# A two-layer diffusion trunk on one core: projections of linear attention placed beside its cores, and modulation steps placed later

## The chip, the cores and the metric

The kernel runs on one core of a Trainium2 chip. Its time is the device time of one execution in microseconds (us); the number compared is the median of several runs. A profile, taken by the hardware on one such execution, goes with it. The engines are TensorE (PE, with its weight loads as PEld), VectorE (DVE), ScalarE (ACT), GpSimd (POOL) and SyncE (SP), which issues every DMA of this kernel.

## The reference

Two transformer layers run over 128 context tokens and 1024 latent tokens of width 1024, all in float32. Each token group has its own conditioning vector, and each layer takes six modulation vectors from it, a shift, a scale and a gate for each of two sub-layers:

```
mod = (jax.nn.silu(cond) @ P['w_mod'][li] + P['b_mod'][li])[:, None, :]
shift1, scale1, gate1, shift2, scale2, gate2 = jnp.split(mod, 6, axis=-1)
h = rms_norm(x, g[0]) * (1.0 + scale1) + shift1
out, new = ab_mix(h, ...) if li % 2 == 0 else diff_mix(h, ...)
x = x + gate1 * rms_norm(out, g[1])
h = rms_norm(x, g[2]) * (1.0 + scale2) + shift2
gate, up = jnp.split(h @ P['w_ffn_in'][li], 2, axis=-1)
f = (jax.nn.silu(gate) * up) @ P['w_ffn_out'][li]
x = x + gate2 * rms_norm(f, g[3])
```

In layer 0, `ab_mix` projects h by one matrix `ab_w_in` into the inputs of two attentions, whose outputs are put side by side and projected by `ab_w_out`. One is a latent attention (MLA) with 8 heads: queries and keys/values come out of low-rank vectors of 384 and 256 by "up-projections" (`mla_w_uq`, `mla_w_ukv`), and each query head has a rotated part of 32 and an unrotated part of 64. The other is a gated linear attention (GLA) with 4 heads of 128, run forwards and backwards over chunks of 64 tokens:

```
cum = jnp.cumsum(g, axis=3)
q_in = q * jnp.exp(cum)
k_in = k * jnp.exp(-cum)
a = jnp.where(mask, jnp.einsum('bhncd,bhnsd->bhncs', q_in, k_in), 0.0)
o_intra = jnp.einsum('bhncs,bhnsv->bhncv', a, v)
u = jnp.einsum('bhncd,bhncv->bhndv', k * jnp.exp(cum_last - cum), v)
# S <- decay * S + u from chunk to chunk; o = o_intra + q_in S
```

Layer 1 uses a differential attention on `c_w_qkv`. A feed-forward of width 2816 follows each attention.

## The kernel before

The kernel is written as a list of operations in program order. Every operation is only recorded (`R.tile`, `act`, `dve`, `pe`, `sp`; `Recorder`, from line 171). A planner then sorts the list (`schedule`, line 334): going forward in its own estimate of time, it takes from all operations that are ready, on every engine, the one that can start first, and among equals the one recorded first. The sorted list is issued in `issue` (line 515), whose line 550 is the one line that the profile shows. So each engine executes its instructions in the planner's order. Where a change moves a recorded step, it moves that step's rank, and the planner does the rest.

Memory is handed out by the planner too. A tile belongs to a class ("W", "E", "C", "U", "S", "M", ...), and a class has a fixed list of places in SBUF or banks in PSUM (lines 600 to 635). In most classes tiles get their places strictly in the order in which they are first used in the recorded program. Classes "C" (8 places) and "ps" (8 banks of PSUM) let a later tile go ahead while more than 3, or more than 1, are free. Classes may lie on the same memory, and a place of one is then held back until the other's earlier tiles have been placed (`try_place`, line 377). Four cases matter here:

- "S", 4 places for the states of the linear attention, and "M", 2 places for rows of modulation weights, are the same 2 KB.
- "Uh" (the normalised activations h, six tiles in blocks 0 to 5), "Uq" (MLA inputs, blocks 0 to 4), "Qm" (the attention's queries and keys, blocks 0 to 3) and "U" (the working tiles of the linear attention, blocks 5 to 8) share the nine blocks "U".
- "W" has 4 places for split weights; while the linear attention runs, constants (`gc`, line 1079) and rotation tables (`rq`, line 1090) hold two of them.
- "E" has 6 places; the linear attention's values and output of a head, and the MLA values' output tiles, take them in recorded order.

Float32 products are done in three passes of a faster format: each operand is split into a high and a low part (`load_w`, line 800, does it for weights: DMA into "st", ScalarE copies the high part, VectorE subtracts), and `mm3` multiplies high by high, high by low and low by high. `dense_m` (line 901) makes one 128 x 384 output from 8 blocks of 128 inputs: 24 matmuls. Three such products (3 groups of 384 tokens) go with each weight load.

Layer 0 runs through these stages:

1. Normalised activations h, with two modulation vectors on TensorE (`mod_on_pe`).
2. Projections of h: the output gates of four GLA heads (line 972), the shared rotated key and the GLA gate inputs, the MLA latents (`latent`, line 1011), queries and keys of the four GLA heads (line 1044, stored to DRAM as `qk_d`), and the GLA values for all heads (line 1057).
3. The GLA cores: for each of 4 heads two directions, `gla_core` (line 1153), each over 3 groups of 384 tokens. A group takes a tile of class "U" for its element work on VectorE and ScalarE, then transposes, small matmuls and a chain over the states in class "S". A head's queries and keys take one more "U" tile (`gla_load`, line 1146). After the two directions, `gla_out` (line 1248) normalises, multiplies by the gate and stores.
4. The MLA up-projections are recorded beside the cores: a list `parts` (line 1259) of seven functions (values, rotated queries in two halves, then four times unrotated queries and keys), of which one is recorded after each of the first seven cores. Their inputs are loaded at lines 1092 to 1101.
5. MLA attention, output projection, feed-forward; then layer 1.

The other modulation vectors are computed on VectorE beside all this. `mod_vectors` (line 768) is a generator: for a vector it makes four quarters, each of 8 loads of weight rows (128 x 256) that are multiplied by the conditioning and summed for both token groups, two at a step, followed by a step that transposes and reduces, with a small product on TensorE (tiles `ma`, `mt`). Ten vectors are chained in `later`, in the order (layer, vector) (0,2), (0,4), (0,3), (0,5), (1,1), (1,0), (1,2), (1,4), (1,3), (1,5). `beside(n)` (line 962) records the next n steps at the place in the program where it is called: before each weight load in stage 2, in the products of the feed-forward (line 1614), in two products of its output projection, and before each weight load of layer 1's queries and keys (`diff_qk`, line 1749).

Of the kernel before, what the change touches and what calls it, by code (L numbers as in the profile page):

```python
# [9 lines left out]
F32 = mybir.dt.float32  # L10
F32R = mybir.dt.float32r
AF = mybir.ActivationFunctionType
# [11 lines left out]
GW = 384  # L24
NG = T // GW
# [5 lines left out]
KEYS = NCTX + 128 + NLAT  # L31
# [549 lines left out]
def kernel(ctx: ExitStack, tc: tile.TileContext, I: dict, O: dict):  # L581
    nc = tc.nc
    pool_ = lambda name, bufs, **kw: ctx.enter_context(tc.tile_pool(name=name, bufs=bufs, **kw))
    R = Recorder(nc, tc)
    act, dve, pool, pe, sp = R.act, R.dve, R.pool, R.pe, R.sp
# [62 lines left out]
    def C(dt=F32):  # L648
        return R.tile(now["C"], [128, now["w"]], dt)


    def copy(out, in_):
        R.record([("act", "activation", (), dict(out=out, in_=in_, func=AF.Copy)),
                  ("dve", "tensor_copy", (), dict(out=out, in_=in_))])
# [65 lines left out]
    t = C()[0:64, 0:128]  # L720
# [79 lines left out]
    def load_w(srcs, nk=KD):  # L800

        st = R.tile("st", [128, KD, 128])
        wid = 0
        for off, s in srcs:
            sp.dma_start(out=st[:, 0:nk, off:off + s.shape[1]], in_=s.rearrange("(k p) c -> p k c", p=128))
            wid = max(wid, off + s.shape[1])
        w = R.tile(now["W"], [128, 2, KD, 128], F32R)
        act.activation(out=w[:, 0, 0:nk, 0:wid], in_=st[:, 0:nk, 0:wid], func=AF.Copy)
        tt(w[:, 1, 0:nk, 0:wid], st[:, 0:nk, 0:wid], w[:, 0, 0:nk, 0:wid], ALU.subtract)
        return w  # L810
# [90 lines left out]
    def dense_m(w, h, g, nk=KD, m=128, n=GW):  # L901
        ps = ps_tile()[:m, :n]
        mm3(ps, [((w[:, 0, k, :m], w[:, 1, k, :m]), (h[g][0][:, k, :], h[g][1][:, k, :])) for k in range(nk)])
        return ps
# [57 lines left out]
    def beside(n=1, after=None):  # L962
        R.after = after
        for _ in range(n):
            next(later, None)
        R.after = None
# [3 lines left out]
    start = len(R.ops) - 1  # L970

    for hd in range(4):
        beside(4, start)
        w = first[hd] if hd < FIRST else load_w([(0, W[:, 2240 + hd * 128:2368 + hd * 128])])
        for g in range(NG):
            t = C()
            act.activation(out=t, in_=dense_m(w, h, g), func=AF.Silu)
            sp.dma_start(out=sg_d[hd][:, g * GW:(g + 1) * GW], in_=t)
# [32 lines left out]
    def latent(m0, nk, n, gname, store):  # L1011
        f = [R.tile("E", [128, T]) for _ in range(nk)]
        for m in range(nk):
            beside(5)
            w = load_w([(0, W[:, (m0 + m) * 128:(m0 + m + 1) * 128])])
            for g in range(NG):
                copy(f[m][:, g * GW:(g + 1) * GW], dense_m(w, h, g))
        for g in range(NG):
            s = slice(g * GW, (g + 1) * GW)
            r = norm_r([f[k][:, s] for k in range(nk)], n)  # L1020
            for k in range(nk):
                t = C()
                dve.scalar_tensor_tensor(out=t, in0=f[k][:, s], scalar=vec(gname, k), in1=r,
                                         op0=ALU.mult, op1=ALU.mult)
                store(g, k, t)
# [15 lines left out]
    latent(3, 2, 256, "mla_g_kv", store_kv)  # L1041


    for hd in range(4):
        for i, col in enumerate((672, 1184)):
            beside(5)
            w = load_w([(0, W[:, col + hd * 128:col + (hd + 1) * 128])])
            for g in range(NG):
                t = C()
                if i == 0:  # L1050
                    act.activation(out=t, in_=dense_m(w, h, g), func=AF.Copy, scale=128 ** -0.5)
                else:
                    copy(t, dense_m(w, h, g))
                sp.dma_start(out=qk_d[hd][:, i, g * GW:(g + 1) * GW], in_=t)


    wv = [load_rows([(lambda st: st, W[kk * 256:(kk + 1) * 256, 1696:2208].rearrange("(k p) c -> p k c", p=128))],
# [31 lines left out]

    rq = R.tile("W", [128, 2, NLAT])  # L1090
    sp.dma_start(out=rq, in_=I["k_rope_mla"])
    qn = []
    for g in range(NG):
        q = R.tile("Uq", [128, 2, 3, GW], F32R)
        for j in range(2):
            sp.dma_start(out=q[:, j].bitcast(F32), in_=qn_d[g][j].rearrange("(k p) t -> p k t", p=128))
        qn.append([q[:, j] for j in range(2)])
    ck = [R.tile("Uq", [128, 2, KEYS], F32R) for k in range(2)]
    for k in range(2):
        for j in range(2):  # L1100
            sp.dma_start(out=ck[k][:, j, :].bitcast(F32), in_=ckv_d[j, k * 128:(k + 1) * 128, :])
    Wq = I["mla_w_uq"].rearrange("a (h c) -> a h c", c=96)
    Wk = I["mla_w_ukv"].rearrange("a (h c) -> a h c", c=128)
    qscale = 96 ** -0.5
# [1 line left out]
    def mla_v():  # L1106
        w = load_rows([(lambda st, k=k: st[:, k].rearrange("p (h c) -> p h c", c=64),
                        Wk[k * 128:(k + 1) * 128, :, 64:128]) for k in range(2)], [2, 512])
        for t in range(KEYS // 128):
            s = slice(t * 128, (t + 1) * 128)  # L1110
            ps = ps_tile()
            mm3(ps, [((ck[k][:, 0, s], ck[k][:, 1, s]), (w[:, 0, k, :], w[:, 1, k, :])) for k in range(2)])
            vt = R.tile("E", [128, 8, 2, 64], F32R)
            p3 = ps.rearrange("p (h c) -> p h c", c=64)
            copy(vt[:, :, 0, :], p3)
            dve.tensor_tensor(out=vt[:, :, 1, :], in0=p3, in1=vt[:, :, 0, :], op=ALU.subtract)
            sp.dma_start(out=vm_d[t], in_=vt.rearrange("p a b c -> p (a b c)").bitcast(F32))

    def mla_q_rope(m):
        w = load_w([(32 * i, Wq[:, 4 * m + i, 64:96]) for i in range(4)], nk=3)  # L1120
        for g in range(NG):
            ps = dense_m(w, qn, g, nk=3)
            t = C()
            for c0, n, j in segs(g):
                if j:
                    act.activation(out=t[:, c0:c0 + n], in_=ps[:, c0:c0 + n], func=AF.Copy, scale=qscale)
                else:
                    b = g * GW + c0 - NCTX
                    rope(ps[:, c0:c0 + n], rq[:, 0, b:b + n], rq[:, 1, b:b + n], t[:, c0:c0 + n], qscale)
            hl_to_dram(t, qro_d[m][:, :, g * GW:(g + 1) * GW])  # L1130
# [125 lines left out]
            tt(t, t, sg, ALU.mult)  # L1256
            sp.dma_start(out=mix_d[4 + hd][:, s], in_=t)

    parts = [lambda: mla_v(), lambda: mla_q_rope(0), lambda: mla_q_rope(1)] + [lambda m=m: mla_nope(m) for m in range(4)]
    for hd in range(4):  # L1260
        ld = gla_load(hd)
        for d in range(2):
            gla_core(hd, d, *ld)
            if parts:
                parts.pop(0)()
        gla_out(hd, ld[2])

    HT = NLAT // 2
# [327 lines left out]
    def ffn_in(h, l):  # L1596
# [15 lines left out]
            return out  # L1612

        def product(w, i, acc, first, last=False):
            if l == 0 and i not in ("21", "T3"):
                beside(1, start)
            on = {} if first else {"skip_group_check": True}
            hi, lo = Th[i]
            for u in range(2):
                c = slice(u * 128, (u + 1) * 128)  # L1620
                for k in range(4):
                    wk, a, b = w[k // 2], hi[k // 2][:, k % 2], lo[k // 2][:, k % 2]
                    with R.group():
                        pe.matmul(acc[u], lhsT=wk[:, 0, k % 2, c], rhs=a, start=first and k == 0, stop=False, **on)
                        pe.matmul(acc[u], lhsT=wk[:, 0, k % 2, c], rhs=b, start=False, stop=False, **on)
                        pe.matmul(acc[u], lhsT=wk[:, 1, k % 2, c], rhs=a, start=False, stop=k == 3, **on)
# [120 lines left out]
        sp.dma_start(out=rd[j], in_=I["k_rope_diff"][:, j, :])  # L1747

    def diff_qk(m):
        beside(3)  # L1750
        w = load_w([(0, W[:, m * 128:(m + 1) * 128])])
        scale = 0.125 if m < 8 else 1.0
        for g in range(NG):
            ps = dense_m(w, h, g)
            t = C()
            for c0, n, j in segs(g):
                if j:
                    act.activation(out=t[:, c0:c0 + n], in_=ps[:, c0:c0 + n], func=AF.Copy, scale=scale)
                    if m >= 8:
                        p2 = ps_tile()  # L1760
                        pe.transpose(p2[:, :128], t[:, c0:c0 + n], ident)
                        o = C()
                        copy(o[:, :128], p2[:, :128])
                        sp.dma_start(out=O["new_diff_k"][:, (m - 8) * 128:(m - 7) * 128], in_=o[:, :128])
                else:
                    b = g * GW + c0 - NCTX
                    rope(ps[:, c0:c0 + n], rd[0][:, b:b + n], rd[1][:, b:b + n], t[:, c0:c0 + n], scale)
            if m < 8:
                hl_to_dram(t, q1_d[m][:, :, g * GW:(g + 1) * GW])
            else:  # L1770
                for c0, n, kc in key_cols(g):
                    hl_to_dram(t[:, c0:c0 + n], k1_d[m - 8][:, :, kc:kc + n])
# [195 lines left out]
```

## Time and profile before

| | us |
|---|---|
| median of 3 runs | 3580.55 |
| lowest and highest | 3577.53, 3583.96 |
| the profiled execution's own time | 3575.52 |
| its span in the profile | 3573.7 |
| PE busy in it | 3255.1 (91%) |
| DVE busy | 2506.9 (70%) |
| ACT busy | 1667.5 (47%) |
| mean granted clock of TensorE | 0.944 |

A profile names operations by their tiles: `psum<-U,W` is a matmul whose operands lie in blocks of classes "U" and "W". Names are those of the blocks, so modulation rows show as `S<-in_w_mod` and their sums as `M<-S,sc,M`. "SPq" is a DMA issue on SyncE. In a timeline, the columns are the start, the time that the line covers, the engine, the operation, and behind "x" how many instructions were merged; in square brackets stands how long the engine was idle before, and for whom it waited.

### The profile page before, as it was taken

The numbers are of one execution on the slowest core, as the hardware profiler recorded it, in microseconds if no ns is written. First come the engines' busy times: TensorE is split into PE (matmuls) and PEld (weight loads), VectorE is DVE, ScalarE is ACT, GpSimd is POOL, SyncE is SP. The second block draws the span as 40 slices with busy tenths as digits, with TensorE's granted clock in tenths as the row PEclk, the third lists the DMA queues.
The fourth block names the chain that finished last, engine by engine and source line by source line (L and its number), as shares of the span: only waits on it lengthen the run. The fifth ranks groups of instructions, "written<-read, shape, count | busy, mean of one in ns | idle before, by whom it ended". The sixth has DMA issues, their size and how long they took to land.

```text
span 3573.7 us, 50213 instructions
## 1 busy us (share of the span) xinstructions
PE 3255.1 (91%) x17145; PEld 2773.8 (78%) x17145; DVE 2506.9 (70%) x5941; ACT 1667.5 (47%) x3244; POOL 407.2 (11%) x443
## 2 busy tenths in 40 slices
PE   7999479999876999999998998899997799998997
PEld 5998358889765888877776997788875588887676
DVE  6764577788788877766787587788868755554477
ACT  6422134466565333333455232788856533333344
POOL 0000000133100000000001000566630000000000
PEclk9999678999987999999998999999998799999999
DMA  5455334743343333355345645456333422225224
GB/s 196 134 181 190 121 104 137 200 103 101 114 144 132 124 116 116 117 204 157 106 134 191 188 148 163 102 147 152 111 108 133 128 95 95 92 92 203 84 89 159
DMA packets 359134, 483.49 MB, mean 135 GB/s; under 512 B 39775, under 2 KB 264094, under 8 KB 358206
## 3 DMA queue, kind: packets, MB, share of 16 engines
q1 hardware_dynamic: 358878, 480.29, 43.4%
q8 instruction: 135, 2.21, 0.3%
q14 instruction: 121, 0.99, 0.1%
HBM read 330.42 MB, written 149.77 MB: 134 GB/s over the span
## 4 chain that ended last, share of the span: by engine, by line
PE 80%; DVE 8%; DMA 4%; ACT 4%; issue 2%; POOL 1%; SPq 0%; DVEq 0%; ACTq 0%; POOLq 0%
PE psum L550 80%; DVE U L550 2%; DVE E L550 1%; DVE W L550 1%; ACT E L550 1%; ACT U L550 1%; DMA S<-in_w_mod 1%; DVE C L550 1%; POOL sm L550 1%; POOL E L550 1%; ACT W L550 1%; DVE M L550 1%; DMA C<-hid_d 0%; DVE st L550 0%; DVE H L550 0%
## 5 line engine op out<-in xcount | busy, mean ns | idle before, releaser
L550 PE MATMUL psum<-U,W 128*128 128x512 f32 (+1 forms) x6010 | 1293.7, 370 | 17.2 <-DVE W L550 9.3
L550 PEld LDWEIGHTS psum<-U,W 128*128 128x128 f32 x6010 | 1086.2, 188 | 158.8 <-DVE W L550 11.1
L550 PE MATMUL psum<-E,E 128*128 128x512 f32 x2520 | 588.2, 394 | 28.1 <-ACT E L550 20.2
L550 PEld LDWEIGHTS psum<-E,E 128*128 128x128 f32 x2520 | 475.2, 190 | 133.3 <-ACT E L550 22.0
L550 DVE TENSOR_TENSOR W<-E,W 128x512 fp32r<-128x512 f32 x352 | 240.4, 690 | 185.3 <-ACT W L550 183.2
L550 ACT ACTIVATE E<-E,sm 128x1152 f32<-128x1152 f32 (+1 forms) x280 | 326.8, 1180 | 55.4 <-DVE sm L550 44.6
L550 PE MATMUL psum<-U,U 128*128 128x384 f32 (+4 forms) x1626 | 336.5, 342 | 11.3 <-DVE E L550 3.4
L550 ACT ACTIVATE E<-C 128x512 fp32r<-128x512 f32 (+3 forms) x337 | 197.2, 611 | 318.6 <-PE psum L550 249.2
L550 POOL TENSOR_TENSOR sm<-sm,mhalf 128x1 f32<-128x1 f32 (+2 forms) x124 | 94.4, 766 | 2163.1 <-DVE sm L550 1984.1
L550 ACT ACTIVATE W<-E 128x512 fp32r<-128x512 f32 x352 | 219.3, 628 | 258.2 <-PE psum L550 197.3
L550 DVE TENSOR_TENSOR E<-C,E 128x512 fp32r<-128x512 f32 (+3 forms) x359 | 228.5, 658 | 149.2 <-ACT E L550 147.5
L550 PE MATMUL psum<-W,U 128*128 128x256 f32 (+1 forms) x1620 | 311.7, 339 | 10.2 <-ACT U L550 3.4
L550 DVE TENSOR_SCALAR_CACHE_REDUCE E<-psum 128x384 f32<-128x384 f32 (+1 forms) x600 | 305.7, 538 | 19.2 <-PE psum L550 13.2
L550 PEld LDWEIGHTS psum<-W,U 128*128 128x128 f32 x1620 | 260.0, 195 | 46.4 <-DVE W L550 6.8
L550 DVE SCALAR_TENSOR_TENSOR M<-S,sc,M 128x256 f32<-128x256 f32 x560 | 245.1, 479 | 68.9 <-DMA S<-in_w_mod 51.2
L550 PEld LDWEIGHTS psum<-U,U 128*128 128x128 f32 (+1 forms) x1626 | 265.0, 191 | 32.4 <-DVE E L550 9.6
L550 ACT ACTIVATE C<-psum 128x512 f32<-128x512 f32 (+5 forms) x311 | 128.3, 434 | 342.5 <-PE psum L550 336.2
L550 ACT ACTIVATE W<-psum 128x384 fp32r<-128x384 f32 (+3 forms) x401 | 195.9, 507 | 181.7 <-PE psum L550 175.5
L550 PE MATMUL psum<-ident,E 128*128 128x128 f32 x1273 | 188.7, 286 | 50.0 <-POOL E L550 18.2
L550 PEld LDWEIGHTS psum<-ident,E 128*128 128x128 f32 x1273 | 150.0, 146 | 76.5 <-POOL E L550 29.8
L550 ACT ACTIVATE U<-psum 128x384 f32<-128x384 f32 (+4 forms) x200 | 94.5, 483 | 198.6 <-PE psum L550 192.0
L550 POOL TENSOR_TENSOR E<-E,E 128x1152 f32<-128x1152 f32 (+1 forms) x72 | 174.6, 2426 | 62.8 <-ACT E L550 57.5
(245 smaller groups left out, 3906.7 us busy)
## 6 DMA issues: line engine op xcount, KB each, us to landing
E<-in_w_ffn_in SPq DMA_DIRECT2D x88, 512.0 KB, 3.8
S<-in_w_mod SPq DMA_DIRECT2D x320, 128.0 KB, 2.3
U<-in_w_ffn_out SPq DMA_DIRECT2D x44, 512.0 KB, 6.6
C<-hs_d SPq DMA_DIRECT2D x88, 256.0 KB, 2.6
U<-k_d SPq DMA_DIRECT2D x64, 320.0 KB, 8.5
C<-hid_d SPq DMA_DIRECT2D x66, 256.0 KB, 2.7
st<-in_c_w_qkv SPq DMA_DIRECT2D x24, 512.0 KB, 4.1
st<-in_ab_w_in SPq DMA_DIRECT2D x21, 512.0 KB, 4.0
```

Source lines behind the costliest of these rows:

```text
L550: getattr(self.real[e], m)(*[res(a) for a in args], **{n: res(a) for n, a in kw.items()})
```

## The change

Steps of modulation vectors are recorded at other places (`beside`): 3 instead of 4 before each of the four gate projections, 6 instead of 5 before each of five latent projections, 10 before each of two query and key projections instead of 5 before each of eight, one in six products of a column block of the feed-forward instead of five, and 4 instead of 3 before four of the sixteen weight loads of layer 1.

Of the queries and keys of the linear attention, only head 0's are projected in stage 2. Those of heads 1, 2 and 3 become the first three entries of `parts`, beside the first three cores. The MLA parts follow beside the five later cores, some two at a time, and the loads of their inputs (`mla_in`) move with them.

```
     for hd in range(4):
-        beside(4, start)
+        beside(3, start)
...
         for m in range(nk):
-            beside(5)
+            beside(6)
...
-    for hd in range(4):
-        for i, col in enumerate((672, 1184)):
-            beside(5)
-            w = load_w([(0, W[:, col + hd * 128:col + (hd + 1) * 128])])
-            for g in range(NG):
...
+    def gla_in(hd, i):
+        w = load_w([(0, W[:, (672, 1184)[i] + hd * 128:(672, 1184)[i] + (hd + 1) * 128])])
+        for g in range(NG):
+            t = C()
+            if i == 0:
+                act.activation(out=t, in_=dense_m(w, h, g), func=AF.Copy, scale=128 ** -0.5)
+            else:
+                copy(t, dense_m(w, h, g))
+            sp.dma_start(out=qk_d[hd][:, i, g * GW:(g + 1) * GW], in_=t)
+
+    for i in range(2):
+        beside(10)
+        gla_in(0, i)
...
-    qn = []
-    for g in range(NG):
-        q = R.tile("Uq", [128, 2, 3, GW], F32R)
...
+    qn, ck = [], []
+
+    def mla_in():
+        for g in range(NG):
+            q = R.tile("Uq", [128, 2, 3, GW], F32R)
+            for j in range(2):
+                sp.dma_start(out=q[:, j].bitcast(F32), in_=qn_d[g][j].rearrange("(k p) t -> p k t", p=128))
+            qn.append([q[:, j] for j in range(2)])
+        for k in range(2):
+            t = R.tile("Uq", [128, 2, KEYS], F32R)
+            for j in range(2):
+                sp.dma_start(out=t[:, j, :].bitcast(F32), in_=ckv_d[j, k * 128:(k + 1) * 128, :])
+            ck.append(t)
...
-    parts = [lambda: mla_v(), lambda: mla_q_rope(0), lambda: mla_q_rope(1)] + [lambda m=m: mla_nope(m) for m in range(4)]
+    parts = [[lambda hd=hd, i=i: gla_in(hd, i) for i in range(2)] for hd in range(1, 4)]
+    parts += [[mla_in, mla_v], [lambda: mla_q_rope(0), lambda: mla_q_rope(1)], [lambda: mla_nope(0)],
+              [lambda: mla_nope(1), lambda: mla_nope(2)], [lambda: mla_nope(3)]]
     for hd in range(4):
         ld = gla_load(hd)
         for d in range(2):
             gla_core(hd, d, *ld)
-            if parts:
-                parts.pop(0)()
+            for p in parts.pop(0):
+                p()
         gla_out(hd, ld[2])
...
         def product(w, i, acc, first, last=False):
-            if l == 0 and i not in ("21", "T3"):
+            if l == 0 and i != "21":
                 beside(1, start)
...
     def diff_qk(m):
-        beside(3)
+        beside(4 if m in (0, 1, 8, 9) else 3)
```

More of the change, by code (lines that the diff above doesn't have):

```diff
@@ L1041 @@
     latent(3, 2, 256, "mla_g_kv", store_kv)
-    for hd in range(4):
-        for i, col in enumerate((672, 1184)):
-            beside(5)
-            w = load_w([(0, W[:, col + hd * 128:col + (hd + 1) * 128])])
-            for g in range(NG):
[L1049 to L1054, printed above, removed]
+    def gla_in(hd, i):
[10 more added lines that the diff above has]
+        gla_in(0, i)
     wv = [load_rows([(lambda st: st, W[kk * 256:(kk + 1) * 256, 1696:2208].rearrange("(k p) c -> p k c", p=128))],
@@ L1091 @@
     sp.dma_start(out=rq, in_=I["k_rope_mla"])
-    qn = []
-    for g in range(NG):
-        q = R.tile("Uq", [128, 2, 3, GW], F32R)
[L1095 to L1101, printed above, removed]
+    qn, ck = [], []
[10 more added lines that the diff above has]
+            ck.append(t)
     Wq = I["mla_w_uq"].rearrange("a (h c) -> a h c", c=96)
```

## The prediction, made before the changed kernel was run

> **What bounds the kernel now.** I read the busy slices of the page first, then the busy time in stretches, then TensorE's waits, then the order of time of SyncE and VectorE in the place that these pointed to. In the slices, TensorE is at 7 to 9 tenths nearly everywhere. A slice is 89.3 us (3573.7 / 40); the deepest hole is the fifth, a 4 from 357 to 447, with a 7 behind it. (The other dip, the 6 from 1072 on, is the start of the feed-forward.)
>
> ```profile
> PE   7999479999876999999998998899997799998997
> ```
>
> Cut at the borders of the program's stages, the hole is this (the columns: stretch, length, busy time and instructions of PE, PEld, DVE, ACT, POOL, granted clock, DMA share, GB/s):
>
> ```profile
> 100.00:300.00 200.00, 200.00 (x1238) 194.31 (x1238) 128.41 (x324) 60.44 (x118) 5.97 (x6) 1.00 0.54 161
> 300.00:352.00 52.00, 52.00 (x241) 41.82 (x239) 22.20 (x56) 9.45 (x22) 1.42 (x3) 1.00 0.61 205
> 352.00:365.00 13.00, 10.46 (x44) 7.73 (x42) 9.68 (x23) 7.73 (x15) 0.76 (x3) 1.00 1.02 325
> 365.00:412.00 47.00, 1.38 (x33) 1.03 (x34) 32.61 (x93) 2.72 (x6) 0.00 (x0) 0.50 0.30 92
> 412.00:472.00 60.00, 52.45 (x266) 42.67 (x265) 34.29 (x87) 20.29 (x45) 0.75 (x3) 0.79 0.35 128
> 472.00:545.00 73.00, 57.33 (x255) 43.33 (x255) 51.32 (x141) 25.11 (x56) 4.38 (x10) 0.67 0.24 76
> 545.00:606.00 61.00, 59.65 (x381) 53.18 (x381) 45.73 (x120) 31.90 (x74) 4.10 (x8) 0.94 0.52 165
> 606.00:672.00 66.00, 59.04 (x342) 52.71 (x342) 44.16 (x129) 25.02 (x57) 6.34 (x12) 0.79 0.70 195
> ```
>
> The projections (to 352) fill TensorE wholly at full clock. Then come 47 us with 1.38 us of matmuls. Then the four heads of the linear attention's cores, where TensorE is granted 0.67 to 0.94 of its clock. What ends the 47 us is the group that finishes a quarter of a modulation vector, and behind it stands SyncE's queue:
>
> ```profile
> PE psum L550 <- DVE mt L550: 47.4, 4, 12.3
> ```
>
> ```profile
> 364.97 41.57 SPq L550 DMA_DIRECT2D S<-in_w_mod  x26
> 409.31 0.33 SPq L550 DMA_DIRECT2D S<-in_state_gla_fwd  x1
> 419.17 0.34 SPq L550 DMA_DIRECT2D out_new_gla_fwd<-S  x1
> ```
>
> The initial state of the first core lands in a place that it shares with the weight rows of the modulation steps, and places are handed out in recorded order. All 16 quarters that were recorded ahead of the cores must be through before the first state may be loaded at 409.31. The work recorded behind the first core, the MLA values, can't fill the hole either: their output tiles come after the core's output tile in the order of the E places, so their sums only fill PSUM.
>
> **The steps that move.** A call of `beside` gives one step, five steps finish a quarter, and the first call only starts the chain. Before: 4x4 + 5x5 + 8x5 = 81 calls, which is 16 quarters. After: 4x3 + 5x6 + 2x10 = 62, which is 12 quarters and the first pair of row loads of the thirteenth. The first layer's second gate thus goes behind the cores (it is needed only after the feed-forward), the three vectors that are due earlier stay ahead. The quarters' ends:
>
> ```profile
> 121.30 0.39 DVE L550 TENSOR_REDUCE mt<-ma 128x8 f32<-128x256 f32 x1
> ...
> 331.96 0.42 DVE L550 TENSOR_REDUCE mt<-ma 128x8 f32<-128x256 f32 x1
> ...
> 410.73 0.42 DVE L550 TENSOR_REDUCE mt<-ma 128x8 f32<-128x256 f32 x1
> ```
>
> First, twelfth and sixteenth: (331.96 - 121.30) / 11 = 19.15 us a quarter while TensorE is full. The pace is not set by the number recorded (five calls stand beside a load of some 12.5 us) but by the two places for rows, so fewer projections don't slow it. Quarter 12 still ends at 332; two more row loads, at 41.57 / 26 = 1.6 us each, and their sums make the first state loadable near 337 instead of 409. Bounds: at the stall's pace (12.3 us a quarter, the longest wait above) from the new end of the projections on, 318; a fifth slower, because the first core's element work then shares VectorE, 349.
>
> **The projections that move.** Six pairs of one weight load and three dense products leave the stretch before 352:
>
> ```profile
> L550 SPq DMA_DIRECT2D qk_d<-U x16: 326/327/602, 204.6 to 301.0; - x16
> L550 SPq DMA_DIRECT2D qk_d<-C x8: 320/327/332, 206.7 to 283.9; - x8
> ```
>
> 24 products are stored between 204.6 and 301.0, 96.4 / 23 = 4.2 us each, so 18 products are 75 us. The value projection then ends at 352 - 75 = 277, and from 277 to 337 the first core waits for its state as now. But now there is cover: the queries and keys of heads 1 and 2 (12 products, 50 us) write C places that are next in order, need no E place, and find two of the W places free, as the MLA weights do now. Head 3's (25 us) come behind the output step of head 0 in the order of the C places, so only what PSUM can hold of them is done early. I count the 60 us as full.
>
> What remains from 337 on, in TensorE time at full clock: the cold matmuls cost more, by these rows of the same 12 small products:
>
> ```profile
> 413.26 3.15 PE L550 MATMUL psum<-U 128*64 128x64 f32 x12 [0.58 <-ACT U L550]
> ...
> 453.76 1.94 PE L550 MATMUL psum<-U 128*64 128x64 f32 x12 [0.58 <-ACT U L550]
> ```
>
> 3.15 / 1.94 = 1.62. With a share 2(1 - clock) of each head cold, the heads' busy 52.45, 57.33, 59.65 and 59.04 become 44, 43, 57 and 49.5: 193 us of work in 260, or 0.74. After: 193, plus 10 that the MLA values did at 352 to 365, plus 75 - 60 of the moved projections: 218. At 0.74 that is 293 us, at the best head's 57 / 61 = 0.93 it is 234. I take 0.78, so 279 us: heads 1 to 3 now have more work beside them, but head 0 loses its MLA values and most of its cover, and lies near the worst head (43 / 73 = 0.59). The cores end at 337 + 279 = 616 instead of 672: 56 us less. With 318 or 349 for the state, the same sum gives 622 and 613: when the state comes matters little, since the waiting time is work.
>
> A rule of the Trainium skill speaks against taking cover from a core: "TensorE: Matmul & The Clock Gate", section "What's actually happening", has the array at half rate after a window of some 3.4 us without work. The granted 0.50 in the empty 47 us agrees; the 1.62 above is less than its 2. By 2 instead of 1.62 a wholly cold head 0, with head 1's 43 us of work, would be estimated at 86 us rather than 70, and the gain would be some 16 us less.
>
> **What else moves.** The MLA inputs, ten loads, go from beside the value projection to behind head 3's projections, since they lie where the normalised activations lie:
>
> ```profile
> U<-qn_d SPq DMA_DIRECT2D x6, 576.0 KB, 5.2
> ...
> U<-ckv_d SPq DMA_DIRECT2D x4, 640.0 KB, 7.1
> ```
>
> 6.0 MB at the 205 GB/s of the stretch from 300 to 352 is 29 us. Queued behind them on SyncE are head 1's gate loads and the next weights; who waits is the MLA values' products, with the second core of head 1 beside them, about 30 us long. I cost this at nothing; without that cover it is up to 29 us.
>
> The four quarters go to the feed-forward (6 steps per column block instead of 5) and, a step each, to four of the sixteen query and key loads of layer 1 (202 steps in all, 201 are needed):
>
> ```profile
> 2000.00:2200.00 200.00, 192.27 (x1141) 189.53 (x1140) 157.03 (x412) 55.13 (x125) 0.00 (x0) 0.98 0.55 167
> 1120.00:1600.00 480.00, 479.38 (x2434) 405.23 (x2434) 351.88 (x634) 179.44 (x315) 0.00 (x0) 1.00 0.40 132
> ```
>
> ```profile
> 1120.00:1600.00 480.00, 88.28 (x220) 1.00 0.40 132
> ```
>
> The last row is VectorE on modulation tiles alone: 11 quarters end in that stretch, 8 us each. Two more make 368 of 480 beside a full TensorE: nothing. The rest, up to two quarters, comes on top of 157 of 200 in layer 1's projections, where TensorE already loses 8 us; between nothing and 16 us, I take 4. Their 32 row loads come with them, each an issue on SyncE like the state's 0.33 us above, ahead of weight loads that have a second place to land in.
>
> **Sum.** -56 + 4 = -52 against the profiled execution's own 3575.5 (its span 3573.7 and 1.8 around it): 3523.5. The median of the runs shown is 3580.6, so 3528. A measurement can tell about 0.2% from no change, 7 us.
>
> **Rivals.** *Better filled* (0.14): heads 1 to 3 all run as head 2 does now; at 0.88 the 218 us take 248, 87 us are saved less the 4, 3498. For it, that head holds two MLA parts in 61 us; against it, head 0 has none.
>
> *Part given back at the end* (0.20): the last MLA part is now recorded behind the last core, and the attention's tiles lie on the MLA inputs.
>
> ```profile
> 634.59 0.62 SPq L550 DMA_DIRECT2D U<-qno_d  x1
> ...
> 672.07 0.34 SPq L550 DMA_DIRECT2D out_new_gla_bwd<-S  x1
> ```
>
> Today the attention's first load goes out 37 us before the last core stores its state. Half of that overlap lost is 19 us, 3547; with the rest of the 16 us on VectorE 3559.
>
> *The cover isn't taken* (0.05): head 1's and 2's projections stick as the MLA values do now (no PSUM bank or C place). Then 278 us of work stand after 337; at 0.78 to 0.85 the cores end at 664 to 693, 3577 to 3606; near no change.
>
> *Slower* (0.09): the activations now stay through head 1's first core, so the core's working tiles have three U places and not four, one of them holding queries and keys. If only one group at a time then runs, each costs its whole chain, from its first activation to its last element step and from the stall's end at 412 to its output:
>
> ```profile
> 359.01 0.58 ACT L550 ACTIVATE U<-psum,vecs 128x384 f32<-128x384 f32 x1 [0.27 <-DMA v_d<-U]
> ...
> 369.18 0.36 DVE L550 TENSOR_TENSOR U<-U 128x192 f32<-128x192 f32 x1
> ...
> 422.57 0.98 ACT L550 ACTIVATE E<-psum 128x384 f32<-128x384 f32 x2 [3.42 <-PE psum L550]
> ```
>
> 10.5 + 11 = 21.5 us, against 260 / 24 = 10.8 a group now. Over the nine groups of heads 0 and half of 1 that is 96 us more, 3624; it decides from 52 / 9 = 5.8 us a group on. Against it: with two tiles in flight a group takes 21.5 / 2 = 10.8, just today's pace. The skill's "Perfetto Trace Analysis", section "Optimization Strategy", reads repeated bubbles as places running out; the hole here is one.
>
> **How the numbers follow.** The forecast has 0.52 (3510 to 3545). Faster by over 0.2%: 0.52 + 0.14 + 0.20 = 0.86; within it 0.05; slower 0.09. The range 3495 to 3566 holds the forecast, the part given back and somewhat over half of the better filled case: some 0.8.
>
> **What would show it.** Right: 12 quarter ends before the first state's load and the four next after 1100; that load near 337 with TensorE busy at clock 1.00 between 277 and 337 on 128x384 products; the last core's state stored near 616; a column block of the feed-forward no longer than now. Wrong: a second hole in TensorE between 277 and 400; groups of the first cores more than 16 us apart; waits on modulation tiles between 2000 and 2200; a gap between the last core and the attention.

## The result, and the profile after

The changed kernel takes 3546.72 us (median; 3544.05 to 3550.6), the kernel before, run beside it, 3580.96 us (3577.53 to 3583.96): ratio 0.9906, 95% interval 0.9888 to 0.9923, so 34 us faster. The profiled execution took 3544.05 us with a span of 3542.2. I had forecast 3528 and a gain of 52.

The slices of the page (now 88.6 us each) show what became of the hole, the 4 that stood fifth in the kernel before; the lower row is the granted clock:

```profile
PE   7996989899959999989999998999996799998997
PEclk9997978999979999999999999999998899999999
```

The fifth digit is a 9; what is left is a 6 in the fourth, from 266 to 354. SyncE's order of time (start, time covered, operation) has the two events that the sum hung on, and the attention's first load:

```profile
338.50 0.33 SPq L550 DMA_DIRECT2D S<-in_state_gla_fwd  x1
...
613.92 0.34 SPq L550 DMA_DIRECT2D out_new_gla_bwd<-S  x1
615.15 0.62 SPq L550 DMA_DIRECT2D U<-qno_d  x1
```

I had said 337 and 616 for the first two. The third has changed its place: before, that load went out 37 us ahead of the last core's store, now 1 us behind it. VectorE's order of time shows the twelfth and the thirteenth quarter on the two sides of the cores, as the text had it:

```profile
336.79 0.42 DVE L550 TENSOR_REDUCE mt<-ma 128x8 f32<-128x256 f32 x1
...
1096.80 0.41 DVE L550 TENSOR_REDUCE mt<-ma 128x8 f32<-128x256 f32 x1
```

Busy time by stretch (stretch, length, then PE, PEld, DVE, ACT, POOL, the granted clock, DMA share, GB/s) shows the second difference:

```profile
277.00:309.00 32.00, 32.00 (x191) 29.86 (x189) 17.57 (x44) 11.32 (x21) 0.51 (x2) 1.00 0.62 192
309.00:337.00 28.00, 0.69 (x17) 0.43 (x16) 18.10 (x48) 1.77 (x5) 0.00 (x0) 0.52 0.36 105
337.00:385.00 48.00, 44.94 (x278) 41.21 (x279) 27.75 (x74) 17.31 (x36) 1.01 (x4) 0.89 0.24 74
385.00:435.00 50.00, 50.00 (x311) 46.52 (x310) 23.37 (x58) 16.82 (x35) 3.55 (x6) 0.97 0.42 126
614.00:660.00 46.00, 39.02 (x234) 37.03 (x233) 28.97 (x93) 18.28 (x38) 7.75 (x7) 0.85 0.90 262
1080.00:1560.00 480.00, 480.00 (x2451) 404.72 (x2450) 363.51 (x677) 185.87 (x327) 0.00 (x0) 1.00 0.41 136
```

From 309 to 337 TensorE stands nearly still again (0.69 us of 28), where I had counted it as full. Its order of time says what was issued last ahead of that, and what it waits for (in square brackets: idle time before, and the releaser):

```profile
307.55 1.55 PE L550 MATMUL psum<-E,W 32*128 32x384 f32 x4
311.87 0.29 PE L550 MATMUL psum<-mt,quarter 128*32 128x4 f32 x8 [2.77 <-ACT M L550]
324.72 0.29 PE L550 MATMUL psum<-mt,quarter 128*32 128x4 f32 x8 [12.56 <-DVE mt L550]
337.26 0.29 PE L550 MATMUL psum<-mt,quarter 128*32 128x4 f32 x8 [12.25 <-DVE mt L550]
340.35 0.80 PE L550 MATMUL psum<-U,S 128*128 128x128 f32 x2 [2.80 <-DMA S<-in_state_gla_fwd]
```

The first row is four gate products (`psum<-E,W`, 384 columns) of groups that have no working tile yet. They need only the gate inputs, so they run early and each keeps a bank of PSUM until its tile comes.

Where the gain went is best seen at points of the program, all from SyncE's rows: T1 the first state's load, T2 the last core's state stored, T3 the load of the MLA attention's eighth head's values, T4 the first weight load of layer 1, T5 the first store behind layer 1's attention (`hb`).

| | T1 | T2 | T3 | T4 | T5 | span |
|---|---|---|---|---|---|---|
| before | 409.3 | 672.1 | 875.4 | 1709.2 | 2747.1 | 3573.7 |
| after | 338.5 | 613.9 | 838.0 | 1669.1 | 2718.0 | 3542.2 |
| difference | -70.8 | -58.2 | -37.4 | -40.1 | -29.1 | -31.5 |

At the end of the cores 58 us are won (forecast: 56). From there to T3, 21 are given back: the attention starts later against the cores. Between T4 and T5, in layer 1's projections and attention, 11 more.

### The profile page after: what moved, and what is told of

Its sections match the earlier page's. It is cut to its first block, busy times and chain, and to the rows that moved or that the text cites. A ratio compares the mean times of both kernels' runs of the same rounds, so it can differ in the third digit from the quotient of the medians.

```text
span 3542.2 us, 50156 instructions
## 1 busy us (share of the span) xinstructions
PE 3246.3 (92%) x17145; PEld 2772.4 (78%) x17145; DVE 2494.1 (70%) x5918; ACT 1675.6 (47%) x3267; POOL 406.1 (11%) x443
## 5 line engine op out<-in xcount | busy, mean ns | idle before, releaser
L550 PE MATMUL psum<-W,U 128*128 128x256 f32 (+2 forms) x1603 | 310.8, 341 | 13.8 <-DVE W L550 5.3
L550 ACT ACTIVATE C<-psum 128x256 f32<-128x256 f32 (+5 forms) x327 | 134.1, 433 | 360.1 <-PE psum L550 343.6
L550 PE MATMUL psum<-W,H 128*128 128x256 f32 (+1 forms) x1120 | 161.5, 296 | 19.3 <-ACT W L550 10.9
```

The source lines that it names most:

```text
L550: getattr(self.real[e], m)(*[res(a) for a in args], **{n: res(a) for n, a in kw.items()})
```

## The experiments

Theory 1: the moved modulation steps bring the gain, since the first state waits for their places; the moved projections bring little, because PSUM's banks are held and because the cores are paced by their own chains. Rival: TensorE's work sets the time, as my sum had it, so the projections in the hole are the gain and the empty 28 us are what is missing. Each ratio is to the kernel before, run on the same chip.

### The two halves of the change

The modulation steps alone, on the kernel before:

```
-        beside(4, start)
+        beside(3, start)
...
-            beside(5)
+            beside(6)
...
-            beside(5)
+            beside(10 if hd == 0 else 0)
...
-            if l == 0 and i not in ("21", "T3"):
+            if l == 0 and i != "21":
...
-        beside(3)
+        beside(4 if m in (0, 1, 8, 9) else 3)
```

> Only the modulation steps are moved as in the change (3, 6, 10 twice, then none before the other six query and key projections; feed-forward and layer 1 as in the change). The projections and the MLA parts stay as before. Theory 1, the steps do it: quarter 12 ends near 332, while the value projection still runs to 352, so the hole of 47 us goes without any cover; the first state is loaded near 353, the cores' last state is stored near 615, the MLA inputs and parts keep their places, so nothing is given back at the start of the attention; about 11 us are lost in layer 1 as in the change. 3535 to 3545, no slower than the whole change. Theory 2, the moved projections do most of it: without them half of the gain at most, 3560 to 3570.

3540.9 us, ratio 0.9894 (0.9878 to 0.9911): the steps alone do as much as the whole change, as theory 1 had it.

```profile
361.02 1.45 SPq L550 DMA_DIRECT2D S<-in_state_gla_fwd  x1
...
628.84 0.34 SPq L550 DMA_DIRECT2D out_new_gla_bwd<-S  x1
```

Here the quarters no longer hold the first state: the twelfth ends at 328.90 and the sums of the next rows at 338.3, while the state is loaded 23 us after that, behind the projections (the last store of the values is issued at 347.88). I had expected it near 353 and the cores' end near 615. The cores end 15 us later than with the projections moved too, but the attention's first load goes out at 593.55, 35 us ahead of that end, and T3 is 831.9, ahead of the 838.0 of the whole change.

The projections alone, with the steps where they were (10 of them before each of the two projections that stay in their stage made 20):

```
+    for i in range(2):
+        beside(20)
+        gla_in(0, i)
...
+    parts = [[lambda hd=hd, i=i: gla_in(hd, i) for i in range(2)] for hd in range(1, 4)]
```

> Only the projections and MLA parts are moved as in the change; all 81 modulation calls stand ahead of the cores as before (20 before each of head 0's two), the feed-forward and layer 1 as before. Theory 1: the first state waits for quarter 16, near 388 at the stall's pace; the hole is some 80 us instead of 47, the cores end near 665, the attention's start gives 20 us back, layer 1 loses nothing: 3580 to 3600, not faster than before. Theory 2: the projections fill the wait, the cores end near 640: 3550 to 3565.

3584.68 us, 1.0019 (1.0006 to 1.0032): no gain. The busy time of the hole:

```profile
300.00:390.00 90.00, 12.97 (x114) 10.88 (x114) 54.96 (x147) 7.24 (x15) 0.00 (x0) 0.56 0.29 88
```

The state is loaded at 387.46, the cores end at 663.26, 9 us sooner than before, and T3 is 10 us later than before. T1 comes 22 us sooner, since the quarters run at the stall's pace from an earlier time on; but the work only left a longer hole behind. So the steps are the gain.

### What was given back at the attention, and in layer 1

The last MLA part ahead of the last core instead of behind it, in the changed kernel:

```
-    parts += [[mla_in, mla_v], [lambda: mla_q_rope(0), lambda: mla_q_rope(1)], [lambda: mla_nope(0)],
-              [lambda: mla_nope(1), lambda: mla_nope(2)], [lambda: mla_nope(3)]]
+    parts += [[mla_in, mla_v], [lambda: mla_q_rope(0), lambda: mla_q_rope(1), lambda: mla_nope(0)],
+              [lambda: mla_nope(1), lambda: mla_nope(2)], [lambda: mla_nope(3)], []]
```

> The change, with head 2's and 3's MLA parts one core earlier: both rotated parts and the first unrotated one beside head 2's first core, then two, then the last one beside head 3's first core and nothing beside the last. Theory: the change gives some 20 us back because the attention's queries and keys lie on the MLA inputs and the last part is done after the last core; with the last part ahead of the last core the attention's first load goes out ahead of the last core's end again, and 10 to 20 us come back: 3526 to 3537. Rival, it is lost otherwise (transfers, a colder TensorE, another order within the attention): 3542 to 3552.

3524.46 us, 0.9853 (0.9834 to 0.9871): 0.0053 below the changed kernel's ratio, 19 us, and just below the range that I had expected. SyncE's order of time:

```profile
584.27 0.61 SPq L550 DMA_DIRECT2D U<-qno_d  x1
...
610.63 0.35 SPq L550 DMA_DIRECT2D out_new_gla_bwd<-S  x1
```

The overlap is back at 26 us and T3 is 815.2, 60 us ahead of before. On top of it, the moved quarters taken wholly by the feed-forward:

```
-            if l == 0 and i != "21":
+            if l == 0:
...
-        beside(4 if m in (0, 1, 8, 9) else 3)
+        beside(3)
```

> The change with its last MLA part ahead of the last core (as in the run before it), and the moved quarters taken wholly by the feed-forward: all seven products of a column block have a step beside them, layer 1's query and key loads three each as before the change. Theory 1 (the 11 us lost between the first load of layer 1 and its first output are VectorE's work on the quarters that went there, while the feed-forward has room): layer 1's stretch goes back to 1038 us, the feed-forward stays, 3513 us (3508 to 3519). Rival (the feed-forward has no room either, since TensorE is full and VectorE comes nearer to it): the 11 us appear there, 3524 us.

3514.22 us (3512.07 to 3517.31), 0.9818 (0.9793 to 0.9843): the fastest of all; below it is "the mended version". From T4 to T5, first the run before it, then this one:

```profile
1649.00:2699.00 1050.00, 974.02 (x5343) 852.11 (x5342) 794.57 (x2263) 596.87 (x1136) 266.66 (x281) 0.96 0.49 141
```

```profile
1063.00:1543.00 480.00, 479.26 (x2459) 403.07 (x2458) 373.31 (x714) 183.91 (x324) 0.00 (x0) 1.00 0.42 140
1652.00:2687.00 1035.00, 967.11 (x5327) 847.76 (x5326) 781.95 (x2225) 592.61 (x1125) 266.40 (x281) 0.97 0.49 141
```

The third busy time is VectorE's: 12.62 us less of it, and the stretch is 15 us shorter (T4 to T5: 1050.5 and 1035.3). Of the feed-forward's 480 us (upper row of the second fence) TensorE still loses less than 1, with VectorE at 373. T3 to T4 is 833.4 and 833.1. The intervals of the two ratios just touch, but T4 to T5 parts all the runs of this document: 1047 to 1050 us in the four that put moved steps into layer 1, 1032 to 1038 in the other ten. So VectorE's work was free in the feed-forward and cost its full length, and a little more, in layer 1.

The same mend with the steps alone (no projection moved):

> The modulation steps alone are moved (no projection), with the moved quarters taken wholly by the feed-forward as in the first run of this list. Theory 1: the run with the steps alone was 3541 us and lost 10 us in layer 1, which come back: 3530 us (3525 to 3537); what the projections beside the cores are worth, once the tail is mended, is the difference to the first run of this list, 10 to 20 us. Rival (the loss in layer 1 isn't from the steps): 3541 us.

Its edit is the feed-forward line of the last diff, on the first experiment's kernel, with three steps at every weight load of layer 1 as before. 3521.9 us (3508.57 to 3525.0), 0.9832 (0.9807 to 0.9858), 3 us below the range that I had expected. What the moved projections are worth after all mends is the difference to 3514.22, 8 us; the two intervals overlap, so it isn't settled that it is more than nothing.

### Is it PSUM that keeps the hole empty, and does filling it pay?

In the changed kernel, each gate product is made to wait until its group has its working tile (a strip of the tile is written first, and the product put behind that):

```
             tmp = R.tile("U", [128, 8, GW])
+            pool.memset(tmp[:, 7, 0:64], 0.0)
+            R.after = len(R.ops) - 1
             ps = ps_tile()[:, :GW]
             pe.matmul(ps, lhsT=wg[32:64, d, hd * 128:(hd + 1) * 128], rhs=misc[32:64, s], start=True, stop=True)
+            R.after = None
```

> The change, with one thing more: the gate product of a core's group is recorded to come after a small clearing write to that group's working tile, so it takes no PSUM bank before the tile has a place. Theory: in the change the hole from 309 to 340 is there because gate products of groups without a working tile, with the first two groups' sums, hold seven of eight banks, so head 2's projections can't start. Then here TensorE is full from 275 to 340, about 28 us of projections are done earlier, and the cores end 15 to 28 us sooner, 3520 to 3532. Rival, the hole is due to the C or W places or to the order of the weights: the hole stays, 3540 to 3550.

3544.27 us, 0.9911 (0.9895 to 0.9926). Busy time by stretch:

```profile
300.00:320.00 20.00, 20.00 (x130) 19.14 (x129) 8.87 (x23) 3.81 (x7) 0.00 (x0) 1.00 0.36 108
320.00:340.00 20.00, 20.00 (x123) 19.73 (x122) 11.77 (x27) 4.38 (x7) 0.00 (x0) 1.00 0.49 143
380.00:460.00 80.00, 59.82 (x231) 46.74 (x231) 35.28 (x90) 20.50 (x44) 4.43 (x12) 0.61 0.21 71
```

Ahead of its tile a gate product takes nothing but a bank, and without the early products the hole is full at full clock: the banks are the reason. But no time is won, a miss for the gain I had expected. The quarters that stood beside the empty TensorE at 12.5 us each now take 16 to 17, the state comes at 350.09 instead of 338.50, and between 380 and 460 TensorE is busy for only 59.82 of 80 us. The cores end at 640.61, 27 us later than in the changed kernel; yet T3 is 839.3, against 838.0 there: the MLA parts are done ahead of that end, and the attention's first load goes out at 611.92. That run also delays every later group's gate product, so it isn't the last word. The same hole filled for the most part in another way, by recording heads 1 and 2 both beside the first core, on the mended version:

```
+    parts = [[lambda hd=hd, i=i: gla_in(hd, i) for hd in (1, 2) for i in range(2)], [],
+             [lambda i=i: gla_in(3, i) for i in range(2)]]
```

> As the first run of this list, but the queries and keys of heads 1 and 2 are both recorded beside the first core (nothing beside the second), so that the gate products of the second core don't stand ahead of head 2's projections for PSUM's banks. Theory 1 (the rest of the hole, 30 us without TensorE work before the first state, is PSUM held by products whose working tile isn't free; but the cores that follow are bound by their own chains, so filling it brings little): TensorE is busy in the hole, the cores end within 8 us of the first run of this list, 3505 to 3520 us. Rival (TensorE's work is what the cores wait for, as I had summed it): 25 us of work done in the hole are 20 to 30 us less in the cores, 3485 to 3495 us.

3519.43 us, 0.9832 (0.9807 to 0.9858), where the mended version has 0.9818 (0.9793 to 0.9843). TensorE is busy for 26.50 of the 38 us up to the state, which comes at 347.48, 9 us later; the cores end at 618.58 instead of 614.31. Two ways to fill the hole, one wholly and one for two thirds, and no gain from either. The Trainium skill, "Perfetto Trace Analysis", section "Optimization Strategy", says that a gap which repeats on an engine that should be saturated can mean too little SBUF or PSUM. The full 300 to 340 above agree with it on the reason; whether the gap is worth anything the rule doesn't say, and here it wasn't.

### How far the first state can be brought forward

Eight quarters ahead of the cores, four beside the MLA attention's heads, on the mended version:

```
-        beside(3, start)
+        beside(2, start)
...
-            beside(6)
+            beside(4)
...
-        beside(10)
+        beside(7)
...
+        beside(3)
```

> On top of the run before it in this list: 42 calls ahead of the cores, which is 8 quarters, and the four quarters taken out stand beside the eight heads of the MLA attention, three steps a head. Theory 1 (what the first core waits for is the place of its state, and every quarter taken away brings it forward until something else does): the first state is loaded near 280 to 300 instead of 338, the cores end some 30 us earlier; VectorE's four quarters, 8 us each, land on the attention, where VectorE is busy 17 of 20 us, so up to 32 us come back there: 3495 to 3520 us. Rival (the cores are bound by their own chain and the values' projection, not by the state's place): the state comes early, the cores end within 10 us of the run before, and the attention is longer: 3520 to 3550 us.

3525.57 us, 0.9836 (0.9808 to 0.9863): theory 1's 3495 to 3520 is missed by 6. The state comes at 298.49, 40 us sooner, and the cores end at 583.52, 31 us sooner. But T3 is 818.6, as without it (818.8), and T4 is 15 us later. From the end of the cores to T3, without and with the four quarters:

```profile
614.00:819.00 205.00, 194.87 (x1368) 181.18 (x1368) 177.52 (x617) 138.32 (x294) 63.78 (x55) 1.00 0.49 130
```

```profile
584.00:819.00 235.00, 208.09 (x1387) 187.91 (x1387) 202.09 (x686) 142.15 (x297) 63.22 (x54) 0.95 0.49 131
```

25 us more on VectorE make the stretch 30 us longer: each early microsecond of the cores was paid with one of the attention up to T3. Of the 15 us behind T3, 11 are lost up to the first store behind this attention (`ha`, at 1006.75 instead of 996.11), where VectorE has 7.07 us more of modulation tiles; the last 4 weren't followed up.

### What paces the cores

Nothing beside the cores: all projections ahead of them, all MLA parts behind, with the steps moved as in the run of 3521.9 us. Nothing is left out, it only stands elsewhere:

```
         for d in range(2):
             gla_core(hd, d, *ld)
-            if parts:
-                parts.pop(0)()
         gla_out(hd, ld[2])
+    for p in parts:
+        p()
```

> The steps alone moved, as in the run with the steps all in the feed-forward, but nothing stands beside the eight cores: all queries and keys are projected ahead of them, and all MLA up-projections (60 us of TensorE work by its rows) come behind the last core. It shows the length of the bare cores, from the first state's load to the last core's stored state; with their MLA parts it was 265 us. Theory 1 (the cores are paced by their own chains between the engines, and other work beside them is nearly free up to what TensorE can hold): the bare cores take 240 to 270 us, with TensorE at a low clock; the whole kernel gets longer by the 60 us that stand behind them, 3570 to 3585 us. Rival (my sum's assumption, that the cores' time is TensorE's work over a share of 0.78): 133 us of work remain, 170 us and up to 210 if they are cold, and the kernel stays near 3520 to 3540 us.

3576.38 us, 0.9996 (0.9982 to 1.001). The bare cores last from 363.55 to 583.73, 220 us: below theory 1's 240 and above the rival's 210. They aren't wholly bare, for recording the parts behind the cores gives them only a later rank: between 510 and 572 the planner put all 60 products of the MLA values (`psum<-W,U`, 512 columns) beside the last two heads, some 16 us by rows of six in 1.63 us. The other end, useless work beside the last four cores of the mended version:

```
+    def extra(m):
+        w = load_w([(64 * i, Wq[:, 2 * m + i, 0:64]) for i in range(2)], nk=3)
+        for k in range(4):
+            for g in range(NG):
+                copy(C(), dense_m(w, qn, g, nk=3))
+    for m in range(4):
+        parts[4 + m] = parts[4 + m] + [lambda m=m: extra(m)]
```

> The change with its last part early and all moved steps in the feed-forward, plus work that nobody needs: beside each of the last four cores one more weight load and twelve more products of 9 matmuls of 384 columns, evicted and dropped, 19 us of TensorE work each, 76 us in all. Theory 1 (chains pace the cores, and work beside them fills gaps and keeps the clock up): of the 76 us some 50 can be taken up, since TensorE has 15 us without work in the 280 us of the cores and loses some 40 more to the low clock there: the cores end 20 to 40 us later, 3535 to 3555 us. Rival (the time is the work over 0.78): 97 us later, 3610 us.

3578.14 us, 1.0000 (0.9981 to 1.0019): 63 us more on the span than the mended version, 50 of them at the cores' end (664.26) and 11 more up to T3, where again a part stood behind the last core. Theory 1's 20 to 40 and the rival's 97 are both missed. The cores' own stretch, in this order: nothing beside them, before, after, the mended version, extra work:

```profile
364.00:584.00 220.00, 188.74 (x985) 153.25 (x986) 146.54 (x401) 76.69 (x168) 14.85 (x32) 0.76 0.19 61
```

```profile
409.00:672.00 263.00, 228.98 (x1247) 192.32 (x1248) 177.87 (x483) 102.32 (x232) 15.58 (x33) 0.79 0.44 138
```

```profile
338.00:614.00 276.00, 257.30 (x1438) 226.20 (x1439) 176.83 (x466) 109.64 (x241) 15.59 (x33) 0.86 0.41 137
```

```profile
339.00:614.00 275.00, 258.74 (x1511) 228.96 (x1512) 181.61 (x480) 113.89 (x251) 15.53 (x34) 0.90 0.49 158
```

```profile
337.00:664.00 327.00, 314.96 (x1855) 286.85 (x1856) 190.39 (x487) 132.60 (x288) 13.44 (x31) 0.93 0.42 139
```

By the prediction's formula, work at full clock = busy x (1 - 2(1 - clock) x (1 - 1 / 1.62)), these are 154, 192, 230, 239 and 298 us of work, in 220, 263, 276, 275 and 327 us: shares of 0.70, 0.73, 0.83, 0.87 and 0.91. The share that I had taken as a constant rises with what stands beside the cores. From end to end, 144 us of work cost 107 us, 0.74 us for one, where my sum charged 1 / 0.78 = 1.28. Of the 37 us saved, 18 are less loss to the low clock (busy less work: 35 us at one end, 17 at the other) and 19 less time without matmuls (31 and 12 us), an estimate by the same formula. The steps between two runs scatter (43 us for 38, 13 for 38, -1 for 9, 52 for 59), so the order counts as well: the two runs that fill the hole take 291 us for 212 (the delayed gate products) and 272 for 223. One more order, heads 1 and 2, then 3, then the MLA parts over five cores:

```
+    parts = [[lambda hd=hd, i=i: gla_in(hd, i) for hd in (1, 2) for i in range(2)],
+             [lambda i=i: gla_in(3, i) for i in range(2)], [mla_in, mla_v],
+             [lambda: mla_q_rope(0), lambda: mla_q_rope(1)], [lambda: mla_nope(0), lambda: mla_nope(1)],
+             [lambda: mla_nope(2)], [lambda: mla_nope(3)], []]
```

> Another order of the same parts: heads 1 and 2 projected beside the first core (which fills the hole, as seen), head 3 beside the second rather than the third, so that the MLA inputs come one core earlier and the MLA parts spread over four cores; the last part still ahead of the last core. Theory 1 (chains pace the cores, the order of what stands beside them matters little): 3505 to 3520 us, within 8 us of the run with the steps all in the feed-forward. Rival (what was lost in the run with two heads beside the first core was the second core's empty side): 3485 to 3500 us.

3525.62 us, 0.9851 (0.9822 to 0.9881): outside both expectations, and on the profiled spans 11 us slower than the mended version's order, though the intervals of the two ratios overlap. The cores take 281 us for 214 us of work by the same formula; which wait makes this order worse wasn't followed up.

Last, the rival "slower" by itself, three U places in all eight cores of the kernel before:

```
-            ("U", bU[5:9], None)
+            ("U", bU[6:9], None)
```

> The kernel before, with three U places for the linear attention's working tiles and its queries and keys instead of four, in all eight cores; nothing else. It is the rival 'slower' of my prediction by itself, taken further: there it held for head 0 and half of head 1. Theory 1 (two working tiles in flight are enough for the pace, since the chain of one group is some 21 us and a group comes every 11): at most 30 us slower, 3580 to 3610 us. Rival (with three places, one of them holding the queries and keys, groups follow one another): 10 us for each of 24 groups, 3820 us; something between if only the heads' borders suffer.

3599.85 us, 1.0062 (1.0043 to 1.0081). The cores take from 407.38 to 702.00, 295 us instead of 263: 1.3 us for each of 24 groups, not 10. With two tiles in flight a group's pace holds almost. The cores end 30 us later and the span grows by 22, so 8 come back behind the cores.

## Why the prediction was right, point by point

- *The quarters and the state's load.* Quarter 12 at 332 and the load near 337: measured 336.79 and 338.50, with the sums of the next pair of rows at 337.59 in between. That the quarters hold the state's place is shown by the two halves of the change: with the steps alone the load moves by 48 us and the time falls, with the projections alone it moves by 22 and the time doesn't. That 332 came out so near is in part luck. The steady 19 us a quarter didn't hold behind the projections' new end: the ninth quarter ends at 274.31, the tenth 37 us later, beside the first core's groups, the last two 13 us apart as in the old stall.
- *The cover from 277 to 337, counted as full.* Failed: 28 of the 60 us are empty. Head 1's products ran, head 2's stuck behind the gate products that hold the banks. That is the rival "the cover isn't taken" in half, and the line "a second hole between 277 and 400" was its right sign. But its price was wrong: filling the hole twice gained nothing.
- *218 us of work at 0.78, 279 us.* By the same formula, measured 230 at 0.83, 276 us. The total is near by luck, for two errors cancel: 230 us at my 0.78 would have been 295. The work: the empty 28 us left 246, and the last MLA part moved behind the cores (8 us: 27 matmuls of 384 columns and 24 of 320, an estimate from 33 of the former in 5.97 us); the other 8 I can't account for. The share isn't a property of the cores: it goes from 0.70 to 0.91 in the five stretches above.
- *MLA inputs at nothing.* Right: their loads go out from 421.62 to 435.3, and TensorE is busy for all of 385 to 435.
- *Feed-forward at nothing.* Right: 480.00 of 480 us on TensorE.
- *Layer 1, +4 of 0 to 16.* Mis-sized: 11 us, and they are the moved steps' (the run with all steps in the feed-forward got all of it back). I had taken VectorE's 157 of 200 for room; the stretch got longer by about what VectorE got to do.
- *The attention's start.* Here the forecast failed as a sum: I had "part given back" as a rival with 0.20, half of the 37 us overlap, 19 us. It was the case: 21 us were lost and the run with the last part early took 20 back. The sign "a gap between the last core and the attention" is there too: TensorE stops for 6.75 us until 633.71, waiting for the load of the attention's keys (`kr_d`). Forecast -56 + 4; measured -58 + 21 - 3 + 11 - 2 = -31 on the profiled spans.
- *Slower by three U places.* Its mechanism exists, at 1.3 us a group instead of 10.8: 12 us at most for the nine groups in question.

One thing stays open: whether the states in memory of their own would let the first core start without waiting for any quarter. It wasn't tried.

## What to carry to other kernels

Before moving work into a hole, find which shared place ends the hole: here the modulation rows held the states' place, and moving the rows was the whole gain, while the projections put beside the cores brought 8 us at best, which the intervals don't settle. When parts are moved back by one position, look at what stood last and what it overlapped: leaving the last position empty was worth 20 us. And a step is only free where its own engine has room beside the bound one: up to two quarters cost nothing in the feed-forward and 11 to 15 us in layer 1, and some four cost 30 us in the attention up to T3 and more behind it.

## What was unexpected of the hardware

Work put beside these cores' chains of small matmuls on TensorE cost, from one end of the runs to the other, less than its own time, 0.74 us for one. One part of it goes with the clock in the rows above: the granted clock rises from 0.76 with the least beside the cores to 0.93 with 144 us more of work. That activity lifts the clock is what the Trainium skill says in "TensorE: Matmul & The Clock Gate", section "What's actually happening", and these rows agree.
